# Later window-value stores and residual loads, a sixth pair of value pages, and a later second bank turn for the norm

## The chip, the cores and the metric

The kernel runs on one core of one Trainium2 chip. Its time is device microseconds for one execution; three timed runs of the kernel before gave 931.88, 934.51 and 935.48 us, and the median of such runs is the metric. The profile is of one further execution, which has its own time (below).

## The reference, cut to what matters

One decoder layer is computed for a prompt of 512 positions and for 8 samples of one new position each, whose past of 2048 positions lies in pages of 128 positions, found by a page table. All arithmetic is float32.

```python
q, q_rot, ck, cv, sk, sv, wk, wv, gate, dq, dk, dv = _project(x, pos, attn_norm, w_in)   # RMSNorm, one projection
o_nsa  = gate0 * compressed + gate1 * selected_blocks + gate2 * sliding_window          # 8 heads
o_diff = rmsnorm(softmax(q1 k1) v - lam * softmax(q2 k2) v) * (1 - lam_init)            # 4 heads
x = x + concat(o_nsa, o_diff) @ w_out
x = x + conv_ffn(x)                                                                     # up, conv of width 3, gate, down
y = rmsnorm(x)
```

For the samples the values of the differential heads and of the selected blocks are read page by page, 8 samples x 16 pages. The sliding window keeps 512 positions for each sample: its old values come in shifted by one, the sample's new value row is put in as the last row, the window is used, and the updated window is an output (`s_win_v`).

## The kernel before, in words

TensorE multiplies float32 matrices as split products (a rounded part and a rest, three matmuls), with the 520 columns (512 prompt, 8 sample) in two halves of 260. The work has these stretches in the profiled execution: the input projection together with the scores against the key pages (tiles `kp`, to 174 us); the compressed branch, fed by pages `cp` (to some 314 us); prompt attention together with the value pages `vp` (some 314 to 480 us); the output projection; the up projection, the convolution and the down projection (to the end), which are written out in a fixed order.

Up to the start of the output projection nothing is ordered by hand. Each piece of work is a small process, a Python generator (`p_...`), that yields what it needs: an event, a turn in a ring of buffers (`Ring`, `Slot`), a pause in microseconds, or an operation with its engine and a cost. `Issue.run` builds the order of the instructions from these: it takes the engine that can start first, and on it the operation that is due first. It rehearses 8 times, each time with due times worked back from the rehearsal before, then tries 60 random variations of the best, and emits the program of the best. So one changed pause or one changed turn can move every instruction before the output projection, on all engines. Once emitted, each engine runs its own list in order.

Names that the change and the steps of the prediction touch:

- `p_vload` loads value pages in pairs (`v_load`, line 527 by the helper `page`) into a ring of `NV` buffers `vp` (2 pages, 320 KB each page). All DMAs before the output stage are issued from SyncE (SP), one list.
- `p_win` handles the sliding windows of the 8 samples in order: load the window (L2044, into one of two halves of `kcT`), pause, put the new row in from `vn` (L2046; it has to wait for the window to have landed), pause, store the window to the output (L2048; it has to wait for the row to have landed).
- `p_v` multiplies the pages: `vc<-PTc` opens a sample, `vp,Sd` are the differential heads, `vp,Ss` the selected blocks, `kcT,Sw` the window. Two samples share the one bank of role `v`; `p_half` empties it (tile `od`).
- `p_main` is the prompt attention: per unit, scores (`z,q` and `z,dq`), softmax on VectorE and ScalarE, transposes of the probabilities (`cst,p`, L1896), products with values (`pt,wh`, `pt,wl`, `pt,dv`, `wo,vcp`), and `p_finish`.
- `p_rms`, used by `p_finish` for each of the four differential heads and once for the samples, sums squares on TensorE (`ones,sq`), scales on VectorE, takes the power on GpSimd (tile `rsm`), and spreads the result by transposes (L557). It needs the two small banks of the ring `MR` once each, `m1` and `m2`. A ring gives its turns strictly in the order in which they were asked for: a turn that was asked for holds back all later ones until it is taken.
- `p_residual` loads four tiles of the residual input `xT` into buffers that prompt attention has done with (L2222).
- `numbers`, `load_w`, `win` and the rings `VS` and `VB` are as the quoted code shows.

```python
MR, VB = Ring(2), Ring(1)          # two small banks; one bank for the pages' sums
VS = Ring(NV)                      # pairs of value pages in flight
VR("vp", [128, 2, 640], F32, NV)   # their buffers
```

Of the kernel before, what the change touches and what calls it, by code (L numbers as in the profile page):

```python
# [415 lines left out]
def build(tc, T, plan, last):  # L416
    with tc.manual_schedule():
        _build(tc, T, plan, last)


def _build(tc, T, plan, last):
# [6 lines left out]
    def act(out, in_, func=AF.Copy, **kw):  # L428
        se.activation(out=out, in_=in_, func=func, **kw)  # L429
# [20 lines left out]
    def flat(ap):  # L450
        return ap.rearrange("p a b -> p (a b)")
# [78 lines left out]
    def rms(pool, ssq, n, nt=NT):  # L530


        ssq = ssq if isinstance(ssq, list) else [ssq]
        p = ps("m")
        blk = [(c, min(128, nt - c)) for c in range(0, nt, 128)]
        nb = len(blk)
        sm = pool("rsm", [128, 2, 5], F32, 2)
        if nt % 128:
            ve.memset(sm, 1.0)
        for j, (c, w) in enumerate(blk):  # L540
            for i, s in enumerate(ssq):
                mm(p[:w, j:j + 1], s[:, c:c + w], ones[:, 0:1], i == 0, i == len(ssq) - 1)
        yield None
        full = sum(w == 128 for _, w in blk)
        for lo, hi, w in ((0, full, 128), (full, nb, blk[-1][1])):
            if hi > lo:
                ve.tensor_scalar(out=sm[:w, 0, lo:hi], in0=p[:w, lo:hi], scalar1=1.0 / n, scalar2=EPS,
                                 op0=OP.mult, op1=OP.add)
        yield None
        tt(ge, sm[:, 1, :nb], sm[:, 0, :nb], mhalf[:, :nb], OP.pow)  # L550
        yield None
        out = []
        for j0 in range(0, nb, 4):
            q = ps("m")
            for j in range(j0, min(j0 + 4, nb)):
                w = blk[j][1]
                te.transpose(q[:, (j - j0) * 128:(j - j0) * 128 + w],  # L557
                             sm[:w, 1, j:j + 1].to_broadcast([w, 128]), ident[:w, :w])
            out.append(q)
        yield out  # L560
# [121 lines left out]
    ACC, KB, SR, MR, OR, VB = Ring(4), Ring(2), Ring(4), Ring(2), Ring(1), Ring(1)  # L682
# [5 lines left out]
    def E(*key):  # L688
        return ev.setdefault(key, Event())
# [978 lines left out]
    def p_window():  # L1668
# [17 lines left out]
                       t[:, j * 128:(j + 1) * 128], b4 == 0, b4 == 3)  # L1686
            yield (("pe", 0.24, f), E("wm", b)) + ((ksl,) if b == 0 else ())
        yield ("act", tact(256), lambda: act(flat(Sw), box["p"][:, 0:256])), ksl.done, E("Sw")
    NV = 5
    PL = {}  # L1690


# [90 lines left out]
    PR = [Ring(n) for n in NPR]  # L1783
    VS = Ring(NV)
    PB, PT, W, O = {}, {}, {}, {}
    wslots, vslots = {}, {}

    def v_load(i):
        t = PL["VR"]("vp", [128, 2, 640], F32, NV)
        for n in range(2):  # L1790
            page(t[:, n], T["vpg"], 128 + 2 * i + n)
        vslots[i] = t
# [179 lines left out]
    def p_finish(i):  # L1972
# [23 lines left out]
        yield ("act", tact(512), f), sl  # L1996
        yield ("dve", tdve(512), lambda: ve.tensor_copy(out=box["t"], in_=o), PS), osl.done
        yield from p_rms(box, box["q"], 128, S)

        def f():  # L2000
# [5 lines left out]
        yield f_sub(ol[4 + r][:, :S], box["t"], f32(oh[4 + r][:, :S]), 512), sl.done, E("o", 4 + r)  # L2006

    def p_rms(box, ssq, n, nt):
        m1, m2 = MR.slot(), MR.slot()
        yield m1  # L2010
        g = rms(at, ssq, n, nt)
        yield ("pe", 0.3, lambda: next(g)), m1
        yield ("dve", 0.2, lambda: next(g), PS), m1.done
        yield ("pool", 0.95, lambda: next(g)),
        yield m2
        yield ("pe", 0.46, lambda: box.update(r=next(g))), m2
        box["m"] = m2
# [16 lines left out]
    def win(b):  # L2034
        return kcT[:, 4 * (b % 2):4 * (b % 2) + 4]

    def p_win():

        yield E("kcT", 1)
        yield E("vn")  # L2040
        for b in range(B):
            if b > 1:
                yield E("vb", b - 2)
            yield ("dma", 0.75, lambda: sy.dma_start(out=win(b), in_=T["winv"][b])),  # L2044
            yield 5.0
            yield ("dma", 0.05, lambda: sy.dma_start(out=win(b)[127:128, 3], in_=vn[b:b + 1, 0])), E("win", b)  # L2046
            yield 4.0
            yield ("dma", 0.75, lambda: sy.dma_start(out=T["swv"][b], in_=win(b))),  # L2048

    def p_v():  # L2050
# [60 lines left out]
        def f():  # L2111
            act(o2[:, 0], box["p"][:, 0:32])
            act(o2[:, 1], box["p"][:, 0:32], AF.Square)
        yield ("act", 0.5, f), sl.done
        yield from p_rms(box, o2[:, 1], 128, 32)
        yield (("dve", 0.2, lambda: stt(o2[:, 2], o2[:, 0], lam[:, 7:8], box["r"][0][:, 0:32], OP.mult, OP.mult)),
               box["m"].done)
# [48 lines left out]
    def p_wo_first():  # L2166
# [12 lines left out]
        for m in range(2):  # L2179
            slots = [VS.slot() for _ in range(2)]  # L2180
            for sl in slots:
                yield sl
                sl.got.t = -50.0
            h, l = prep["o", m] = [PL["VR"]("vp", [128, 2, 640], F32R, NV).rearrange("p a b -> p (a b)")[:, 0:1024]
                                   for _ in range(2)]
# [27 lines left out]
    def p_residual():  # L2213

        yield E("outs")
        for m, t, e in ((0, T_SV, E("V", "w")), (1, T_WV, E("V", "w")), (2, T_SK, E("exp", NU - 2, 1, 3)),
                        (3, T_WK, E("exp", NU - 1, 1, 3))):
            yield e

            def f():  # L2220
                xs[m] = P(f"z{t}", [128, NT])
                sy.dma_start(out=xs[m], in_=T["xT"][m])  # L2222
            yield ("dma", 0.8, f),
# [39 lines left out]
    for f, prio in ((p_stage2(), 0), (p_load(), 0), (p_w1v(), 0), (p_split(), 1), (p_product(), 3), (p_group("k"), 2), (p_group("v"), 2), (p_scores(), 2), (p_wload(), -1), (p_window(), 1),  # L2263
                    (p_turned(), 5), (p_vn(), 5), (p_nsa(0), 1), (p_nsa(1), 1), (p_cmp_sample(0), 1),
                    (p_cmp_sample(1), 1), (p_switch(), 0), (p_outs(), -3),
                    (p_vload(), 0), (p_win(), -1), (p_main(), 3),
                    (p_values(), 2), (p_pc(), 2), (p_seq(p_scale, range(NU)), 1),
                    (p_seq(p_turn, range(NU)), 1), (p_seq(p_pv, range(NU)), 0),
                    (p_seq(p_dv, [i for i in range(NU) if units[i][0] == "d"]), 3),
                    (p_seq(p_finish, [i for i in range(NU) if units[i][0] != "s"]), 1), (p_v(), v_prio),  # L2270
                    (p_wo_first(), 4),
                    (p_wo(), 4), (p_residual(), 4),
                    (p_out(0, 0, VB, "v"), 7)):
        Q.spawn(f, prio)
# [271 lines left out]
REHEARSALS, VARIANTS = 8, 60  # L2546
# [27 lines left out]
```

## Time and profile before

| | us |
|---|---|
| median of three runs | 934.51 |
| the profiled execution | 932.64 |
| its span | 930.9 |
| TensorE busy in it | 902.6 (97%) |
| VectorE busy | 572.6 (62%) |
| ScalarE busy | 387.9 (42%) |
| GpSimd busy | 159.5 (17%) |
| waits of TensorE that have a named cause, all stretches | 21.2 |

The span is the stretch that the instructions cover, and 1.7 us of the execution lie around it. TensorE is busy nearly always, so what can be won or lost is in its gaps and in its clock: each row of a table by windows gives, after the busy times, the clock that the throttle granted (1.00 is 2.4 GHz, 0.50 is 1.2 GHz), then the mean busy share of the 16 DMA engines and their rate in GB/s. In a row of a timeline, the first number is the start and the second the length of a merged group; a bracket is the time that the engine had stood before it, and whom it waited for. Matmuls overlap, so lengths of neighbours are not added; the distance of their starts is used.

### The profile page before, as it was taken

To read this page: it belongs to the slowest core of one execution; us is meant where nothing else is said; L and a number is where in the kernel's file an instruction comes from. 1 tells how busy PE (TensorE), PEld (TensorE's weight loads), DVE (VectorE), ACT (ScalarE), POOL (GpSimd) and SP (SyncE) were. 2 spreads that over 40 slices of the span, in tenths; PEclk is the share of its full clock that TensorE was granted. 3 is DMA by queue.
4 is the path that set the end of the run, shared out by engine and by line. 5 is a ranking of instruction groups with operands and counts; after the bars stand their busy time and mean duration, and the time that the engine had idled before them with its cause. 6 is when DMAs were issued, how large, how long until landed. Compare 5 with 4: busy or idle time off the path is not lost.

```text
span 930.9 us, 22292 instructions
## 1 busy us (share of the span) xinstructions
PE 902.6 (97%) x8628; PEld 806.6 (87%) x8628; DVE 572.6 (62%) x1360; ACT 387.9 (42%) x802; POOL 159.5 (17%) x332
## 2 busy tenths in 40 slices
PE   8999999999999999999999999999999999999996
PEld 5998888799999765565569999999999999999996
DVE  7696663365776777776763758777777777321133
ACT  5257331365554665544472234444444444211220
POOL 4220210000100000000012532112111111223230
PEclk9999999989999999999999999999999999999998
DMA  7759999996765689888833332222222222433322
GB/s 262 238 203 343 350 361 348 315 314 214 237 221 179 238 304 345 312 286 306 317 124 134 115 114 92 91 92 91 93 93 97 95 93 72 148 104 106 116 75 93
DMA packets 86061, 179.84 MB, mean 193 GB/s; under 512 B 10049, under 2 KB 28994, under 8 KB 85954
## 3 DMA queue, kind: packets, MB, share of 16 engines
q1 hardware_dynamic: 85954, 178.41, 55.7%
q8 instruction: 68, 1.11, 0.5%
q14 instruction: 39, 0.32, 0.1%
HBM read 165.78 MB, written 12.59 MB: 192 GB/s over the span
## 4 chain that ended last, share of the span: by engine, by line
PE 86%; DMA 6%; SPq 2%; DVE 2%; issue 2%; ACT 1%; POOL 0%; POOLq 0%; DVEq 0%
PE bank L426 83%; DMA vp<-in_vpg 3%; PE bank L1896 2%; DMA kcT<-vn 2%; SPq L527 2%; DMA cp<-in_cpg 1%; DVE xl L438 1%; DMA kp<-in_xT 1%; PE bank L557 0%; DVE y L438 0%; DVE wl L435 0%; ACT gh L429 0%; SPq L625 0%; PE bank L1707 0%; POOL rsm L441 0%
## 5 line engine op out<-in xcount | busy, mean ns | idle before, releaser
L426 PE MATMUL bank<-gl,wh 128*128 128x260 f32 x704 | 199.2, 283 | 0.0
L426 PE MATMUL bank<-gh,wl 128*128 128x260 f32 x704 | 199.1, 283 | 0.0
L426 PE MATMUL bank<-gh,wh 128*128 128x260 f32 x704 | 199.0, 283 | 0.0
L429 ACT ACTIVATE wh<-wr 128x1024 fp32r<-128x1024 f32 (+2 forms) x94 | 96.9, 1031 | 188.3 <-PE bank L426 156.1
L435 DVE TENSOR_TENSOR wl<-wr,wh 128x1024 fp32r<-128x1024 f32 (+1 forms) x86 | 109.5, 1273 | 96.3 <-ACT wh L429 96.0
L426 PEld LDWEIGHTS bank<-gh,wh 128*128 128x128 f32 x704 | 132.7, 188 | 0.0
L426 PEld LDWEIGHTS bank<-gh,wl 128*128 128x128 f32 x704 | 132.6, 188 | 0.0
L426 PEld LDWEIGHTS bank<-gl,wh 128*128 128x128 f32 x704 | 132.6, 188 | 0.0
L426 PE MATMUL bank<-xh,wh 128*128 128x260 f32 (+1 forms) x368 | 105.0, 287 | 1.1 <-ACT wh L429 1.1
L426 PE MATMUL bank<-xl,wh 128*128 128x260 f32 (+1 forms) x368 | 103.9, 284 | 2.2 <-DVE xl L438 2.2
L426 PE MATMUL bank<-xh,wl 128*128 128x260 f32 x352 | 99.6, 283 | 0.0
L426 PE MATMUL bank<-hh,wh 128*128 128x260 f32 (+2 forms) x340 | 96.4, 284 | 0.0
L426 PE MATMUL bank<-hh,wl 128*128 128x260 f32 (+2 forms) x340 | 96.2, 283 | 0.0
L426 PE MATMUL bank<-hl,wh 128*128 128x260 f32 (+2 forms) x340 | 96.1, 283 | 0.0
L426 PEld LDWEIGHTS bank<-xh,wh 128*128 128x128 f32 (+1 forms) x368 | 68.3, 186 | 6.8 <-issue 4.5
L438 DVE SCALAR_TENSOR_TENSOR c<-u,cvw,c 128x536 f32<-128x536 f32 x88 | 69.5, 791 | 2.8 <-ACT c L429 1.3
L426 PEld LDWEIGHTS bank<-xl,wh 128*128 128x128 f32 (+1 forms) x368 | 68.4, 186 | 3.0 <-DVE xl L438 3.0
L426 PEld LDWEIGHTS bank<-xh,wl 128*128 128x128 f32 x352 | 66.4, 189 | 0.1
L435 DVE TENSOR_TENSOR wl<-cp,wh 128x256 fp32r<-128x256 f32 x127 | 47.3, 428 | 29.1 <-ACT wh L429 28.8
L426 PEld LDWEIGHTS bank<-hh,wh 128*128 128x128 f32 x340 | 64.1, 189 | 0.1
L426 PEld LDWEIGHTS bank<-hh,wl 128*128 128x128 f32 x340 | 64.1, 189 | 0.0
L426 PEld LDWEIGHTS bank<-hl,wh 128*128 128x128 f32 x340 | 64.0, 188 | 0.0
(390 smaller groups left out, 1910.5 us busy)
## 6 DMA issues: line engine op xcount, KB each, us to landing
vp<-in_vpg SPq DMA_DIRECT2D x128, 320.0 KB, 5.4
kp<-in_kpg SPq DMA_DIRECT2D x128, 256.0 KB, 5.2
cp<-in_cpg SPq DMA_DIRECT2D x128, 192.0 KB, 3.9
wr<-in_w_up SPq DMA_DIRECT2D x44, 512.0 KB, 3.2
wr<-in_w_in SPq DMA_DIRECT2D x21, 512.0 KB, 5.4
wr<-in_w_down SPq DMA_DIRECT2D x16, 512.0 KB, 3.4
out_zT<-z SPq DMA_DIRECT2D x14, 260.0 KB, 5.5
wr<-in_w_down SPq DMA_DIRECT2D x8, 384.0 KB, 3.1
```

Of the source, the lines that this page charges most:

```text
L426: te.matmul(out, l, r, start=start, stop=stop)
L429: se.activation(out=out, in_=in_, func=func, **kw)
L435: eng.tensor_tensor(out=out, in0=a, in1=b, op=OP.subtract)
L438: ve.scalar_tensor_tensor(out=out, in0=a, scalar=s, in1=b, op0=o0, op1=o1, **kw)
L527: sy.dma_start(out=dst, in_=src[bass.ds(numbers[k][i - k], 1)].rearrange("o p f -> (o p) f"))
L1896: te.transpose(p[:, j * 128:(j + 1) * 128], PB[i, g, q][0][:, k * 128:(k + 1) * 128], ident)
```

## The change

Four edits and what comes of them. The store of a sample's window values waits 10 us instead of 4 us in the plan before it is queued. The ring of value pages has six pairs instead of five. The norm asks for its second small bank after the power instead of together with the first. Residual loads wait 6 us in the plan. A rehearsal that gets stuck no longer throws its plan away for the next.

```diff
-    NV = 5
+    NV = 6
@@ p_rms
-        m1, m2 = MR.slot(), MR.slot()
+        m1 = MR.slot()
         yield m1
         g = rms(at, ssq, n, nt)
         yield ("pe", 0.3, lambda: next(g)), m1
         yield ("dve", 0.2, lambda: next(g), PS), m1.done
         yield ("pool", 0.95, lambda: next(g)),
+        m2 = MR.slot()
         yield m2
         yield ("pe", 0.46, lambda: box.update(r=next(g))), m2
@@ p_win
             yield ("dma", 0.05, lambda: sy.dma_start(out=win(b)[127:128, 3], in_=vn[b:b + 1, 0])), E("win", b)
-            yield 4.0
+            yield 10.0
             yield ("dma", 0.75, lambda: sy.dma_start(out=T["swv"][b], in_=win(b))),
@@ p_residual
             yield e
+            yield 6.0
@@ kernel
-            if k < REHEARSALS:
+            if k < REHEARSALS and p.plan:
                 plan = p.plan
```

Since the order is planned anew, it differs on all five engines up to the output projection; the amount of work is the same. Three places matter.

The list of SP, at the window of the second sample: from its new row (`kcT<-vn`) to the store of that window and the next load. Before:

```order
L2046 DMA kcT_2629<-vn_2640 1x16x8
...
L527 DMA vp_5580<-in_vpg 128x640
...
L527 DMA vp_5600<-in_vpg 128x640
L2048 DMA out_swv<-kcT_2629 128x512
L2044 DMA kcT_2629<-in_winv 128x512
```

Now:

```order
L2047 DMA kcT_2629<-vn_2640 1x16x8
...
L527 DMA vp_5396<-in_vpg 128x640
...
L527 DMA vp_5558<-in_vpg 128x640
L2049 DMA out_swv<-kcT_2629 128x512
L2045 DMA kcT_2629<-in_winv 128x512
```

Each buffer number stands for two page loads, and of the six buffers from vp_5396 to vp_5558 the first and the last are shown. Four page loads stood between the row and the store; now twelve do, for the first five samples alike, four or eight for the last three. Before, it was 8, 4, 8, 4, 10, 4, 6 and none.

The list of TensorE, at the first value pages. `w1vh`, `w1vl` are the last products of the compressed branch, `ce` a small step of the samples' compressed branch, `z10,q0` the first scores of prompt attention. Before:

```order
L426 MATMUL bank5_5000<-kcT_2629,Qzc_81 32x128 x4
L1639 MATMUL bank4_5013<-cst_63,Sw_2635 128x128
L426 MATMUL bank4_5013<-tr_2644,cst_63 128x32
L426 MATMUL bank5_5027<-w2v_2637,hy_4945 128x64 x2
L426 MATMUL bank0_5033<-z10_91,q0_73 128x512
L426 MATMUL bank1_5034<-z10_91,q0_73 128x512
L426 MATMUL bank6_5043<-vc_2630,PTc_2633 32x128
L426 MATMUL bank6_5043<-vp_4794,Sd_103 32x128 x8
L426 MATMUL bank6_5043<-vp_4857,Sd_103 32x128 x8
```

Now:

```order
L1639 MATMUL bank4_4957<-cst_63,Sw_2635 128x128
L426 MATMUL bank4_4957<-tr_2644,cst_63 128x32
L426 MATMUL bank5_4960<-kcT_2629,Qzc_81 32x128 x4
L426 MATMUL bank6_4967<-vc_2630,PTc_2633 32x128
L426 MATMUL bank6_4967<-vp_4841,Sd_103 32x128 x8
L426 MATMUL bank6_4967<-vp_4901,Sd_103 32x128 x8
L426 MATMUL bank6_4967<-vp_4841,Ss_2634 32x128 x2
L426 MATMUL bank6_4967<-vp_4901,Ss_2634 32x128 x2
L426 MATMUL bank6_4967<-vp_4926,Sd_103 32x128 x8
L426 MATMUL bank1_4766<-wh_4773,w1vh1_2656 128x256
```

The first pages were multiplied after all products and after the first unit's scores; now they stand ahead of the last three products and of all scores.

The list of TensorE, at the norm of the last differential head, between its sums of squares (`ones,sq1`) and the transposes of its result (`cst,rsm`). Before:

```order
L426 MATMUL bank5_7340<-ones_67,o2_7307 32x1
L426 MATMUL bank3_7346<-wo_4792,vcp_2631 64x512 x2
L426 MATMUL bank3_7346<-pt_7304,wh_4770 64x512
L426 MATMUL bank3_7346<-pt_7328,wh_4770 64x512
L557 MATMUL bank4_7362<-cst_63,rsm_7341 128x32
L426 MATMUL bank5_7370<-ones_67,sq1_7322 128x1 x4
L557 MATMUL bank4_7385<-cst_63,rsm_7371 128x128 x4
```

Now:

```order
L426 MATMUL bank4_7307<-ones_67,sq1_7288 128x1 x4
L426 MATMUL bank6_6796<-vp_7228,Sd_103 32x128 x8
L426 MATMUL bank6_6796<-vp_7197,Ss_2634 32x128 x2
L426 MATMUL bank6_6796<-vp_7228,Ss_2634 32x128 x2
L426 MATMUL bank3_7331<-wo_4840,vcp_2631 64x512 x2
L426 MATMUL bank3_7331<-pt_7250,wh_4818 64x512
L426 MATMUL bank3_7331<-pt_7314,wh_4818 64x512
L1896 MATMUL bank5_7346<-cst_63,p1_7123 128x128
...
L557 MATMUL bank4_7351<-cst_63,rsm_7308 128x128 x4
```

Nothing stood between the sums and the transposes; now a page, value products and three transposes (one is shown) do, and the transposes use the other small bank, which the norm no longer holds back.

## Rows read from the trace of the kernel before

**Rows 1.** The page: busy time of TensorE, share of the span, instructions.
```profile
PE 902.6 (97%) x8628; PEld 806.6 (87%) x8628; DVE 572.6 (62%) x1360; ACT 387.9 (42%) x802; POOL 159.5 (17%) x332
```

**Rows 2.** Waits of TensorE over the whole span: total us, times, longest us.
```profile
PE bank L426 <- DMA vp<-in_vpg: 3.8, 10, 0.7
PE bank L557 <- POOL rsm L441: 2.5, 2, 1.4
...
PE bank L426 <- DMA cp<-in_cpg: 1.5, 1, 1.5
...
PE bank L426 <- DVE od L438: 1.2, 1, 1.2
...
PE bank L426 <- DVE nsc L441: 1.0, 1, 1.0
PE bank L1896 <- DVE t L438: 1.0, 2, 0.5
```

**Rows 3.** Table by windows of 2 us, 186 to 190 us.
```profile
186.00:188.00 2.00, 2.00 (x9) 0.67 (x9) 1.38 (x3) 1.25 (x4) 0.00 (x0) 0.50 1.03 398
188.00:190.00 2.00, 2.00 (x9) 1.85 (x9) 1.30 (x6) 1.63 (x5) 0.00 (x0) 0.50 1.06 388
```

**Rows 4.** Timeline of TensorE, second and third group of key pages.
```profile
69.55 2.80 PE L426 MATMUL bank<-kp,Qzd 128*32 128x256 f32 x48
...
80.42 2.80 PE L426 MATMUL bank<-kp,Qzd 128*32 128x256 f32 x48
```

**Rows 5.** Table by windows of 2 us, 318 to 322 us.
```profile
318.00:320.00 2.00, 2.00 (x10) 1.67 (x10) 1.97 (x11) 1.18 (x6) 0.00 (x0) 0.50 1.06 408
320.00:322.00 2.00, 2.00 (x11) 0.89 (x10) 0.87 (x2) 0.87 (x5) 0.00 (x0) 0.67 0.81 289
```

**Rows 6.** Timeline of TensorE, last key products of the compressed branch, first value pages.
```profile
302.44 0.29 PE L426 MATMUL bank<-wl,w1h 128*128 128x256 f32 x1
302.56 0.29 PE L426 MATMUL bank<-wh,w1l 128*128 128x256 f32 x1
...
325.09 0.30 PE L426 MATMUL bank<-vc,PTc 128*32 128x128 f32 x1
...
325.24 1.02 PE L426 MATMUL bank<-vp,Sd 128*32 128x128 f32 x28
...
326.34 1.01 PE L426 MATMUL bank<-vp,Sd 128*32 128x128 f32 x28
```

**Rows 7.** Timeline of SP: start, length, DMAs issued.
```profile
306.76 5.71 SPq L527 DMA_DIRECT2D vp<-in_vpg  x10
...
352.16 0.53 SPq L2046 DMA_DIRECT2D kcT<-vn  x1
352.89 2.51 SPq L527 DMA_DIRECT2D vp<-in_vpg  x4
357.75 0.35 SPq L2048 DMA_DIRECT2D out_swv<-kcT  x1
```

**Rows 8.** The page's DMA issues: KB each, median us to landing.
```profile
vp<-in_vpg SPq DMA_DIRECT2D x128, 320.0 KB, 5.4
```

**Rows 9.** Table by windows of 10 us, 350 to 390 us.
```profile
350.00:360.00 10.00, 8.71 (x96) 4.36 (x93) 8.07 (x28) 5.69 (x18) 0.00 (x0) 1.00 1.03 390
...
380.00:390.00 10.00, 8.75 (x109) 4.16 (x101) 5.36 (x18) 3.59 (x9) 0.00 (x0) 1.00 0.92 303
```

**Rows 10.** Groups of TensorE by line, 325 to 488 us: count, busy us, mean ns.
```profile
L1896 PE MATMUL bank<-cst,p 128*128 128x128 f32 x199 | 34.1, 290 | 1.2 <-DVE t L438 1.0 <-ACT pt L429 0.2
L426 PE MATMUL bank<-z,q 64*128 64x512 f32 (+3 forms) x114 | 21.5, 468 | 0.0
...
L426 PE MATMUL bank<-pt,wh 128*64 128x512 f32 (+3 forms) x64 | 11.9, 476 | 0.0
```

**Rows 11.** Timeline of TensorE, norm of the last differential head.
```profile
474.51 1.05 PE L426 MATMUL bank<-ones,sq 128*128 128x1 f32 x8
476.99 0.65 PE L557 MATMUL bank<-cst,rsm 128*128 128x128 f32 x4 [1.43 <-POOL rsm L441]
```

**Rows 12.** Table by windows of 2 us, 478 to 482 us.
```profile
478.00:480.00 2.00, 1.52 (x8) 1.19 (x8) 1.65 (x3) 0.98 (x2) 0.48 (x1) 0.59 0.08 29
480.00:482.00 2.00, 2.00 (x11) 0.93 (x12) 0.90 (x2) 1.94 (x5) 0.00 (x0) 0.56 0.00 0
```

## The prediction

> **What bounds the kernel now.** I read the page first: TensorE is busy for 902.6 us, 97% of the span, and no other engine above 62% [rows 1]. The amount of work does not change, so the time can change only through gaps of TensorE, through its clock, or through the place of work that would otherwise be waited for. The list of TensorE's waits says how much there is [rows 2]: value pages 3.8 us in ten waits of at most 0.7, the power of the norm 2.5 in two, the bank that holds the pages' sums (`od`) 1.2, a small step of the selected blocks (`nsc`) 1.0, the bank behind the norm (`t`) 1.0, the first compressed pages 1.5. Then I read the tables by windows for the clock. Behind three of the longer gaps TensorE runs at 1.2 GHz for a while: behind the wait for compressed pages [rows 3], behind the wait for `nsc` [rows 5], and behind the norm of the last head [rows 12]. At a granted 0.50 a stretch of 2 us does 1 us of work less, so the second fall costs 2 x 0.50 + 2 x 0.33 = 1.7 us and the third 2 x 0.41 + 2 x 0.44 = 1.7 us. Only these stretches, from the end of the key pages to the end of prompt attention, hold anything that the change can reach; the feed-forward part is written out and stays.
>
> All sums are against the profiled execution, 932.64 us, which is span 930.9 and 1.7 around it. It lies 1.9 us under the median of 934.51; I apply the difference to the median.
>
> **The change part by part.**
>
> *Stores set back.* In the list of SP the store of a window waits for the new row to land. Row and store show it: the row goes out at 352.16, four pages follow until 355.40, and the store leaves only at 357.75; nothing behind it leaves either [rows 7]. With twelve pages ahead of the store this hold goes, since at 5.71 us for ten issues [rows 7] twelve take 6.9 us even when no buffer holds them, longer than the 5.4 us that a page takes to land [rows 8]. What is late next is the buffer of a page, not the queue. The window half that is stored is needed again two samples later, so the later store holds nobody. The residual tiles are first needed in the output projection, behind all pages; their pause costs nothing, and one landing of 5.4 us [rows 8] if that cover went.
>
> *Six pairs.* Two more pages can be under way, 12 for 10. Beyond the 3.8 us of page waits [rows 2] this can win nothing directly. I count all 3.8 as gone where SP is the cause, and set a new cost against it.
>
> *Pages start earlier.* The order has them ahead of the last products. The last product that holds their first buffer starts at 302.56; before, the first page was issued 4.2 us later [rows 6, 7] and used at 325.24. Now, by the rows of the list, TensorE reaches the first page after 45 more products at 0.12 us [rows 6], 5.4 us, and ten small groups of about 0.5 us, so 10.3 us behind that product. From there to the end of the third sample stand 48 pages at 1.10 us for four [rows 6], 13.2 us, and between them 30 score matmuls at 2 x 21.5 / 114 = 0.38, 37 transposes at 34.1 / 199 = 0.17, 14 value products at about 2 x 11.9 / 64 = 0.37 [rows 10] (the trace counts scores and value products twice), and some 3 us of small steps: 13.2 + 11.3 + 6.3 + 5.2 + 3 = 39 us. TensorE alone would be through at 49.3 us. The pages: a rate of 390 GB/s makes 0.84 us of the 320 KB, one of 303 GB/s makes 1.08 [rows 8, 9]. The lower one was measured while a store held SP, the higher one at a full DMA share, so I take 0.90. First landing at 0.3 + 5.4, 47 more at 0.90, and three windows in and out, 0.5 MB each, 1.4 us each: 52.2 us. That is 2.9 us behind TensorE, of which I count 2.5 as waits; at 0.84 it is nothing, at 1.08 it is 12.4 us. Net for the value pages: -3.8 + 2.5 = -1.3 us.
>
> The Trainium skill, DMA: Bandwidth & Descriptors, section Bandwidth, puts the memory's share for one core at about 358 GB/s when both cores of a pair stream, as a limit below the fabric's. By it a page takes 0.92 us and the three windows 1.5 each, 53.4 us in all, 1.2 us more of waiting. The windows with 388 to 408 GB/s [rows 3, 5] are above it, so the trace doesn't agree with it as a limit here, where one core runs.
>
> *Gap at the start of prompt attention.* The chain of the selected blocks now has its steps among the products: between the two small transposes that `nsc` stands behind lie twelve products and four transposes, 1.9 us, where six products, 0.7 us, lay. The wait of 1.0 [rows 2] goes, and with it, I think, the 1.7 us of lower clock: -2.7. The bound on the other side is 0, if the page waits make the clock fall in the same place.
>
> *Samples' bank.* Samples 2 and 3 share a bank with 0 and 1, which must be emptied. Before, nothing stood between; now the transpose of the window and three others do, about 0.9 us: -0.8 of 1.2 [rows 2].
>
> *Norm.* From the sums of squares of the last head to its transposes the chain took 2.48 us, 1.43 of them idle [rows 11]. Now a page, four value products and three transposes stand there, some 3.4 us by the same rows: the wait of 1.4 goes. The wait for `t`, 0.5, goes where the transposes use the other bank. The fall of the clock, 1.7, should go too. That is 3.6; I take 3.0, since the last heads' other transposes still follow softmax closely. The other norms of the heads had no wait.
>
> *First compressed pages.* Behind the last key page now stand 42 projection matmuls for 33, 1.1 us more cover for the wait of 1.5 [rows 2]. But the first key pages are used 30 matmuls, 3.6 us, later, and between the second group and the first only 65 stand for 80: pages that came 10.9 us apart [rows 4] must come a little faster. From -1.1, with the clock's fall of at least 2.0 us [rows 3] as much again, to +2; I take -0.5.
>
> *What the new order brings with it.* A planned order never fits the chip quite; the waits that I take away were of this kind. In the old order they were `od` 1.2, `nsc` 1.0, `t` 1.0 and the norm 1.4 [rows 2], 4.6 us, and I expect as much of others in the new one.
>
> Sum: -1.3 - 2.7 - 0.8 - 3.0 - 0.5 + 4.6 = -3.7 us. 932.64 becomes 928.9, and the median 934.5 becomes 930.8.
>
> **The rivals.**
>
> The new order is as good as it looks: no other waits come, -8.3, 926.2 us. For it: most of the named gaps get more cover than they were long. Against it: every order of this planner has small waits.
>
> The waits only move: what goes here returns elsewhere, to 8.3 us, 934.5 us. For it: no work is removed, and TensorE is at 97%. Against it: the queue's hold and the ring's hold are real and go.
>
> Slower: the page supply becomes the bound at the start. Place: the first three samples, where TensorE would like 48 pages in 39 us. At 303 GB/s [rows 9] the waiting is 12.4 in place of 2.5, so -3.7 + 9.9 = +6.2, 940.7 us. It decides from about 1.00 us a page, where the waiting reaches 7.2 us and the gain is eaten up. For it: DMA share 1.03 with the rate at 390 [rows 9], there is no more to be had. Against it: the store no longer stops the queue, and the samples that follow have more other work between their pages.
>
> The clock falls at the pages. In the trace page waits of up to 0.7 us leave the granted clock at 1.00 [rows 2, 9], and falls came only behind gaps of 1.0 us or more. Now more pages lie one behind the other at the start, and three falls of 1.7 us would make -3.7 + 5.1 = +1.4, 935.9 us. The Trainium skill, TensorE: Matmul & The Clock Gate, section HAM oscillation, describes bursts of matmuls between DMA waits where every burst starts at the lower clock; so far the trace does not agree for the short waits.
>
> **How the numbers follow.** My forecast has 0.40, with a range of its own of 928 to 933.5. As good as it looks 0.20, waits only move 0.22, page supply 0.10, clock at the pages 0.08. A measurement of this kernel can tell 0.5%, 4.7 us, from no change: faster means under 929.8, slower over 939.2. Faster are all of the second case and nearly half of the first, 0.37; slower is most of the page supply, 0.09; the rest, 0.54, is no change. The range leaves out a tenth on either side: 925 to 938.5.
>
> **What would show it.** Right: the store of a window leaves without SP standing, no wait of a microsecond or more for the norm's power before the output projection, a granted clock of 1.00 at the start of prompt attention and at its end, page waits of 2 to 3 us together, mostly for the first three samples. Wrong: page waits over 7 us, a fall of the clock between the first pages and the fourth sample, or key pages waited for in the input projection.

## The result, and the profile after

The changed kernel took 922.84 us, the median of four runs (921.75 to 925.21), beside 933.91 us of the kernel before (931.88 to 935.48): a ratio of 0.9885, with a 95% interval of 0.9856 to 0.9914. That is 11 us less. The forecast was 930.8 us with a range of 925 to 938.5: the direction was right, but the time lies below the range. Four far slower executions among the experiments below, of 1241 to 3013 us, are left out of their ratios.

The profiled execution took 923.06 us, with a span of 921.2 us, 9.7 less than before. The page of the changed kernel, busy times as in [rows 1]:

```profile
PE 899.1 (98%) x8628; PEld 805.7 (87%) x8628; DVE 573.5 (62%) x1362; ACT 384.4 (42%) x790; POOL 168.3 (18%) x342
```

The work of TensorE is the same (8628 matmuls), its busy time 3.5 us shorter. Its waits after, beside [rows 2] (total us, times, longest):

```profile
PE bank L426 <- DVE z L441: 1.4, 2, 1.2
...
PE bank L426 <- DMA cp<-in_cpg: 1.3, 2, 1.0
...
PE bank L426 <- ACT p L429: 1.1, 1, 1.1
PE bank L426 <- DMA kp<-in_kpg: 1.0, 2, 0.8
PE bank L557 <- POOL rsm L441: 1.0, 1, 1.0
...
PE bank L426 <- DMA vp<-in_vpg: 0.8, 3, 0.4
PE bank L426 <- DVE od L438: 0.5, 1, 0.5
...
PE bank L426 <- DVE nsc L441: 0.2, 1, 0.2
```

Value pages fell from 3.8 to 0.8, the power of the norm from 2.5 in two waits to 1.0 in one (that of the last norm of the whole kernel, at 914 us, is left), `od` from 1.2 to 0.5, `nsc` from 1.0 to 0.2, and `t` is gone. New are 1.1 for the probabilities of the first scores (`p`, 0.2 before) and 1.0 for key pages. The whole list adds up to 15.2 us, against 21.2 before.

SP after, at the window of the second sample, which [rows 7] shows before: start, length, DMAs issued.

```profile
338.46 0.54 SPq L2047 DMA_DIRECT2D kcT<-vn  x1
340.25 8.84 SPq L527 DMA_DIRECT2D vp<-in_vpg  x12
349.13 0.43 SPq L2049 DMA_DIRECT2D out_swv<-kcT  x1
349.61 0.43 SPq L2045 DMA_DIRECT2D kcT<-in_winv  x1
```

Twelve pages follow the row, and the store leaves right behind the last: SP no longer stands at it. TensorE at the start of prompt attention, first value pages and what it waited for, beside [rows 6]:

```profile
307.66 0.28 PE L426 MATMUL bank<-wh,w1l 128*128 128x256 f32 x1
...
318.92 0.30 PE L426 MATMUL bank<-vp,Sd 128*32 128x128 f32 x3
...
326.55 0.42 PE L426 MATMUL bank<-vp,Sd 128*32 128x128 f32 x8 [0.17 <-DMA vp<-in_vpg]
327.36 0.43 PE L426 MATMUL bank<-vp,Sd 128*32 128x128 f32 x8 [0.39 <-DMA vp<-in_vpg]
328.90 1.13 PE L426 MATMUL bank<-z,q 64*128 64x512 f32 x4 [1.11 <-ACT p L429]
```

The first page is multiplied 11.3 us behind the last `w1l` product (318.92 - 307.66). The three gaps in brackets make 1.7 us together. The table by windows of 2 us, with the columns of [rows 3, 5, 12], at the places that these show: compressed branch, start and end of prompt attention.

```profile
186.00:188.00 2.00, 0.95 (x7) 0.51 (x6) 0.00 (x0) 0.96 (x1) 0.00 (x0) 0.71 0.98 340
188.00:190.00 2.00, 2.00 (x9) 0.96 (x9) 1.76 (x5) 0.88 (x5) 0.00 (x0) 0.50 1.03 403
...
318.00:320.00 2.00, 2.00 (x52) 1.96 (x52) 0.47 (x3) 0.63 (x3) 0.00 (x0) 1.00 1.04 406
...
326.00:328.00 2.00, 1.23 (x32) 0.42 (x21) 1.85 (x12) 0.99 (x5) 0.00 (x0) 1.00 0.96 312
328.00:330.00 2.00, 1.10 (x8) 0.35 (x11) 1.93 (x7) 0.84 (x4) 0.00 (x0) 1.00 0.90 298
...
478.00:480.00 2.00, 2.00 (x17) 1.75 (x15) 0.00 (x0) 0.92 (x2) 0.00 (x0) 1.00 0.00 0
```

The fall behind the compressed pages is still there; those at the start and the end of prompt attention are gone. The table by windows of 10 us, beside [rows 9]:

```profile
330.00:340.00 10.00, 9.82 (x171) 6.98 (x170) 9.69 (x44) 7.60 (x27) 0.93 (x1) 1.00 1.03 383
...
350.00:360.00 10.00, 10.00 (x144) 6.03 (x142) 8.20 (x27) 4.20 (x13) 0.00 (x0) 1.00 0.99 376
...
380.00:390.00 10.00, 10.00 (x149) 6.74 (x147) 7.02 (x25) 5.08 (x16) 1.87 (x3) 1.00 0.68 225
```

In the last two TensorE is busy without a gap, and by 380 the pages are ahead: the share of the DMA engines is 0.68 where it was 0.92. A page still takes 5.5 us to land (median; 5.4 before [rows 8]). The norm of the last differential head on TensorE, start and length, beside [rows 11]:

```profile
463.05 0.95 PE L426 MATMUL bank<-ones,sq 128*128 128x1 f32 x8
...
466.97 0.60 PE L557 MATMUL bank<-cst,rsm 128*128 128x128 f32 x4
```

The chain now has 3.9 us and TensorE does not stand. Of the groups of [rows 10] the transposes show best that the work itself costs what it did (count, busy us, mean ns, idle before):

```profile
L1896 PE MATMUL bank<-cst,p 128*128 128x128 f32 x200 | 33.6, 286 | 0.5 <-ACT pt L429 0.3 <-DVE pt L1910 0.2
```

They cost 286 ns each for 290, with 0.5 us of waits for 1.2.

The up projection starts at 527.0 us, 536.9 before, so the whole gain lies ahead of it. For each kernel below I added up, from windows of 2 us up to that start, the time in which TensorE was not busy (idle) and the busy time times one minus the granted clock (clock):

| stretch, us | before: idle + clock | after: idle + clock |
|---|---|---|
| 0-60 | 5.0 + 0 | 4.6 + 1.5 |
| 60-200 | 1.5 + 3.0 | 2.3 + 3.1 |
| 200-300 | 0.2 + 0 | 0 + 0 |
| 300-340 | 1.9 + 1.7 | 2.2 + 0 |
| 340-460 | 6.0 + 0 | 1.5 + 0 |
| 460-500 | 2.5 + 1.5 | 1.5 + 0 |
| 500 on | 2.8 + 0 | 1.4 + 0 |
| sum | 19.8 + 6.2 | 13.5 + 4.6 |
| rest (busy, at full clock) | 510.9 | 508.9 |

So 6.3 us of idle time, 1.6 of lower clock and 2.0 of busy time make the 9.9.

### The profile page after: what moved, and what is told of

It reads as the page before. It is cut to its first block, busy times and chain, and to the rows that moved or that the text cites. A ratio compares the mean times of both kernels' runs of the same rounds, so it can differ in the third digit from the quotient of the medians.

```text
span 921.2 us, 22310 instructions
## 1 busy us (share of the span) xinstructions
PE 899.1 (98%) x8628; PEld 805.7 (87%) x8628; DVE 573.5 (62%) x1362; ACT 384.4 (42%) x790; POOL 168.3 (18%) x342
## 3 DMA queue, kind: packets, MB, share of 16 engines
q8 instruction: 68, 1.11, 0.5%
## 4 chain that ended last, share of the span: by engine, by line
PE 89%; DMA 4%; DVE 3%; issue 2%; SPq 1%; ACT 1%; POOL 0%; POOLq 0%; DVEq 0%
PE bank L426 85%; PE bank L1896 3%; DMA kp<-in_kpg 2%; SPq L527 1%; DMA kcT<-vn 1%; DVE bank L1835 1%; DMA cp<-in_cpg 1%; DMA wr<-in_w_in 0%; PE bank L557 0%; DMA vp<-in_vpg 0%; DVE y L438 0%; PE bank L1707 0%; DVE wl L435 0%; ACT gh L429 0%; ACT xh L429 0%
## 5 line engine op out<-in xcount | busy, mean ns | idle before, releaser
L441 DVE TENSOR_TENSOR u<-bank,rst 128x260 f32<-128x260 f32 x132 | 40.0, 333 | 38.6 <-PE bank L426 33.0
```

The costliest lines, as they stand in the source:

```text
L441: eng.tensor_tensor(out=out, in0=a, in1=b, op=op)
```

## The experiments

The planner makes a new order after every edit. So the first question is what an edit is worth, and what the order that was drawn happens to be worth. All ratios are to the kernel before, on the same chip.

**One edit at a time.** Each kernel is the one before with one of the four edits and the line on the stuck rehearsal (by itself that line leaves the program as it was, word for word); the edits are those of the diff of the change, one at a time, as here in store_alone:

```diff
-            yield 4.0
+            yield 10.0
             yield ("dma", 0.75, lambda: sy.dma_start(out=T["swv"][b], in_=win(b))),
```

> Theory 1, each edit removes its own hold: TensorE's page waits fall from 3.8 us to about 1.5, SP's hold at the window stores from 10.2 us to under 2, the norm's wait of 1.4 and the lower clock at the end of prompt attention stay; 931 us against 933.9. Theory 2, the new time is a draw of the planner, whatever the edit: the time lies anywhere from 926 to 938, and waits that the edit doesn't touch (start of prompt attention, norm) move as much as those it touches.

> Theory 1, each edit removes its own hold: SP's hold at the window stores stays at some 10 us, but two more pages in flight hide part of it, page waits 3.8 to about 2.5 us; the norm's wait and the fall of the clock at the end stay; 932.5 us against 933.9. Theory 2, a draw of the planner: anywhere from 926 to 938, with the untouched waits changed as well.

> Theory 1, each edit removes its own hold: the wait for the power ahead of the output projection (1.4 us), the one behind it (0.5) and the fall of the clock there (1.5) go, page waits stay at 3.8; 930.5 us against 933.9. Theory 2, a draw of the planner: anywhere from 926 to 938, page waits and the start of prompt attention changed too.

> Theory 1, each edit removes its own hold: a load that is needed 30 us later is moved, so nothing: 933.9 us, within 1. Theory 2, a draw of the planner: the order differs on all engines, so the time lies anywhere from 926 to 938; a change of 3 us or more here can only be the draw.

| kernel | us | ratio | 95% |
|---|---|---|---|
| store_alone | 927.28 | 0.9928 | 0.9904 to 0.9952 |
| six_alone | 930.87 | 0.9970 | 0.9949 to 0.9991 |
| norm_alone | 928.77 | 0.9938 | 0.9919 to 0.9957 |
| resid_alone | 929.52 | 0.9947 | 0.9922 to 0.9971 |

All four are faster, 2.2% taken together, nearly twice what they give in common. Even the pause of the residual loads, for which SP stands 4.8 us with and without it, "gives" 0.5%. In all four the norm of the last head is no longer waited for, edited or not: only the 1.0 of the kernel's last norm is left. So that wait belonged to the one order of the kernel before. What looks like an edit's own effect is the page supply. Page waits are 1.2 us in store_alone and 1.6 in six_alone, lower than was expected of either, but 5.6 in norm_alone and 3.2 in resid_alone, where 3.8 would have stayed. In store_alone the stores hold SP for 2.8 us, in six_alone for 15.3 in seven waits. The row of SP's waits in the kernel before (total us, times, longest):

```profile
SPq L2048 <- DMA kcT<-vn: 10.2, 4, 3.8
```

the same row in store_alone:

```profile
SPq L2048 <- DMA kcT<-vn: 2.8, 1, 2.8
```

and in six_alone:

```profile
SPq L2048 <- DMA kcT<-vn: 15.3, 7, 2.9
```

But the gap for `nsc` is larger with three of the edits alone, 2.0 us in store_alone, six_alone and norm_alone, and 1.4 in resid_alone, where before had 1.0.

**Other draws of the same kernel.** The random variations of the planner get another seed, once with the source of before and once with that of after:

```diff
-    rng = np.random.default_rng(0)
+    rng = np.random.default_rng(1)
```

> The kernel before with another seed of the planner's random variations, no edit. Theory 1, each edit removes its own hold, and the order before is a fair one: within 2 us of the kernel before, and the norm's wait stays. Theory 2, the order before was a poor draw: clearly faster, 928 to 932 us, without the norm's wait and with the window store still holding SP for 10 us or more, as in the four single edits.

> As with the other seed. Theory 1: within 2 us of the kernel before. Theory 2: 928 to 932 us, and the norm's wait gone; the two seeds differ from each other by 1 to 3 us.

> The kernel before, another seed. If the order before was a poor draw and the edits are worth little: 927 to 932 us, as the first two other seeds (932.0 and 928.5) and the single edits. If the order before was typical: 933 to 936 us.

> As the seed before it: 927 to 932 us if the order before was a poor draw, 933 to 936 us if it was typical.

> The changed kernel with another seed. Theory 1: within 2 us of the changed kernel's 922.8, page waits about 1 us. Theory 2, if the changed order was also a good draw: 924 to 929 us. A mixture is likeliest: the edits are worth some 4 us between the means of the seeds, the draw of the kernel before the rest.

> As with the other seed: theory 1 within 2 us of 922.8, theory 2 from 924 to 929 us; page waits about 1 us and no store that holds SP by both.

> The changed kernel, another seed. If the edits are worth some 3 us by themselves: 924 to 928 us, and the mean over the seeds of the changed kernel stays some 3 us under that of the kernel before. If only the draw counts: 927 to 932 us, as its first two other seeds (929.0 and 929.8), and the means over the seeds without the first come together.

> As the seed before it: 924 to 928 us if the edits are worth some 3 us by themselves, 927 to 932 us if only the draw counts.

| seed | before: ratio (95%) | lost, us | after: ratio (95%) | lost, us |
|---|---|---|---|---|
| 0 (as given) | 1 | 26.0 | 0.9885 (0.9856 to 0.9914) | 18.1 |
| 1 | 0.9963 (0.9943 to 0.9984) | 27.8 | 0.9946 (0.9924 to 0.9967) | 19.1 |
| 2 | 0.9934 (0.9914 to 0.9954) | 23.4 | 0.9951 (0.9926 to 0.9976) | 22.8 |
| 3 | 0.9976 (0.9952 to 1.0000) | 25.2 | 0.9946 (0.9926 to 0.9966) | 22.6 |
| 4 | 0.9978 (0.9958 to 0.9999) | 24.0 | 0.9946 (0.9918 to 0.9974) | 21.6 |

"Lost" is idle plus clock from the table's method, one profile for each. The four other seeds have a mean of 0.9963 without the edits and 0.9947 with them. So, as a bookkeeping by these means, of the 1.15%, 0.37% (3.4 us) is that before's own order is worse than its other draws, 0.16% (1.5 us) is the edits on draws that nobody chose, and 0.62% (5.8 us) is that the changed kernel's own order is better than other draws of the same source. Seed 2 alone even stands the other way round (0.9934 and 0.9951), so 0.16% is not certain to differ from zero.

The profiles say where edits and draw part. From 300 to 340 us the loss is 3.3 to 8.6 us on the five orders without the edits and 1.1 to 2.2 on the five with them; from 460 to 500 us it is 0.7 to 4.0 and 0 to 1.5. These two stretches go with the edits: the gap for `nsc` (0.3 to 2.0 us without) shows on none of the four other seeds with them. How they close it is not shown. It is not by the stores alone, which hold SP for 9.0 to 13.9 us without the edits and for 0 to 4.1 with them: in store_alone they hold it for 2.8 us, and 6.1 us are still lost from 300 to 340 us. Part is given back in two places: 200 to 300 us has 1.3 to 1.8 on the other seeds with the edits (0.2 to 0.7 without), and 340 to 460 us has 4.6 to 5.9 (3.3 to 6.0 without). Of these ten only the order of the changed kernel has 1.5 there. On average over seeds 1 to 4, 6.5 us are won in the first two stretches and 2.7 given back in the other two. All in all the lost time falls by 3.6 us (25.1 to 21.5), and the up projection starts 2.4 us earlier. That is more than the 1.5 us of the ratios, so that the edits' own worth stays uncertain by a microsecond or more. Page waits, without the edits 3.8, 5.0, 2.4, 3.4 and 2.6 us, are 3.7, 3.9, 2.8 and 3.2 on the other seeds with them, where about 1 was expected, and 0.8 in the changed kernel alone.

**The due times kept.** The last emission takes other settings than the rehearsals, so the due times stay and only what the edit itself moves differs:

```diff
-    NV = 6
+    NV = OPT["pairs"]
...
+BEFORE = dict(pairs=5, store=4.0, resid=0.0, late=False)
+AFTER = dict(pairs=6, store=10.0, resid=6.0, late=True)
...
+        OPT.update(dict(AFTER, pairs=5) if k == REHEARSALS + VARIANTS else AFTER)
```

(The pauses and the turn of the norm read `OPT` in the same way; shown is newplan_five, and the last line is what differs between the five.)

oldplan_edits is before's due times with all edits; newplan_plain is after's due times with none; newplan_store4, newplan_early and newplan_five take back one edit each (the store's pause, the late turn of the norm, the sixth pair).

> The search is made for the kernel before, and only the program that is emitted has all edits, at the due times of that plan. If the edits are worth something by themselves: page waits from 3.8 to about 1.5 us, the window stores hold SP no more, 931 to 932 us against some 934.8. If only the draw counts: the waits at the start of prompt attention and at the norm stay with the plan, 934 to 935 us.

> The search is made for the changed kernel, and the emitted program has none of the edits. If the edits are worth something by themselves: stores hold SP for 10 us again, page waits 3 us and more, some 3 to 4 us over the changed kernel's 922.8, so 926 to 927. If only the draw counts: within 1 us of 922.8, because start of prompt attention and norm keep the order of that plan.

> The changed kernel's plan, with the store's pause alone put back to 4 us in the emitted program. If the store is what the edits are worth: SP held for 8 us or more at the stores, page waits 2 us and more, 925 to 926 us. If only the draw counts: within 1 us of 922.8.

> The changed kernel's plan, with the norm asking for both banks at once in the emitted program. If the norm's turn counts by itself: transposes wait behind its second turn for the power, 1 to 2 us for each of four heads, of which some 2 us show, 925 us. If only the draw counts: within 1 us of 922.8, and no wait for the power before the output projection.

> The due times that the changed kernel ended with, all of its edits but one: five pairs of value pages in place of six. Theory (the gain hangs on the exact order, and any small disturbance of it loses some 5 us): 0.993 to 0.996, TensorE's lost time between 340 and 460 us back at 3 to 6 us from 1.5. Rival (each edit has its own steady worth, and the sixth pair is worth the 0.3% that it had alone): 0.991 to 0.992.

| kernel | us | ratio | 95% | lost, us |
|---|---|---|---|---|
| oldplan_edits | 930.99 | 0.9954 | 0.9930 to 0.9977 | 24.4 |
| newplan_plain | 929.16 | 0.9954 | 0.9940 to 0.9968 | 21.8 |
| newplan_store4 | 928.97 | 0.9948 | 0.9926 to 0.9969 | 21.6 |
| newplan_early | 927.51 | 0.9942 | 0.9921 to 0.9963 | 21.4 |
| newplan_five | 928.15 | 0.9929 | 0.9912 to 0.9945 | 24.6 |

At the due times of before, the edits do much of what they were made for: in oldplan_edits no store waits for its row any more, page waits are 2.4 us for 3.8, and neither the norm of the last head nor `t` is waited for. The waits for `nsc` (1.0) and `od` (1.2) stay with the plan. That is worth 0.46%, about as the first of its two expectations had it.

At the due times of after, the first three kernels (newplan_five came later) came out slower than either of their expectations, which went up to 927 us for newplan_plain, 926 for newplan_store4 and 925 for newplan_early. Taking back any one of the three edits that were tried loses 0.4 to 0.6%, and taking back all four 0.7%. (The pause of the residual loads was not tried alone.) If each had a worth of its own, three of them would already make 1.6%. So their worths do not add, and each is needed for the time of this order. That what is lost is the fit of the order, which any of them disturbs, is the likeliest reading, but it is not shown: no run disturbs these due times without taking back an edit. For the store at least it is not the hold of SP that comes back. With the pause at 4 us and these due times, six loads still stand between row and store for the first sample and ten for the next four, and no store waits for its row, where 8 us of hold or more was expected. SP in newplan_store4 at the second sample:

```profile
336.73 0.51 SPq L2048 DMA_DIRECT2D kcT<-vn  x1
337.43 8.48 SPq L527 DMA_DIRECT2D vp<-in_vpg  x10
345.96 0.43 SPq L2050 DMA_DIRECT2D out_swv<-kcT  x1
```

Its up projection starts 6.9 us later than in the changed kernel: 3.5 of these are lost time, most of it from 300 to 340 us (2.6), and 3.4 are busy time at full clock.

In newplan_five one can see a cause. TensorE's waits for value pages in it (total us, times, longest):

```profile
PE bank L426 <- DMA vp<-in_vpg: 5.0, 7, 1.9
```

and in the changed kernel, run beside it:

```profile
PE bank L426 <- DMA vp<-in_vpg: 1.0, 3, 0.5
```

The timeline of SP in newplan_five ahead of the longest of them (start, length, DMAs issued):

```profile
427.96 0.75 SPq L2206 DMA_DIRECT2D wo<-in_w_out  x1
436.31 3.89 SPq L527 DMA_DIRECT2D vp<-in_vpg  x6
```

its timeline of TensorE at that wait:

```profile
442.10 0.43 PE L426 MATMUL bank<-vp,Sd 128*32 128x128 f32 x8 [1.89 <-DMA vp<-in_vpg]
```

and its table by windows behind it (the granted clock is the third number from the end):

```profile
442.00:444.00 2.00, 1.90 (x13) 1.11 (x15) 0.56 (x1) 0.00 (x0) 0.00 (x0) 0.64 0.99 368
444.00:446.00 2.00, 2.00 (x7) 0.51 (x3) 0.65 (x3) 0.00 (x0) 0.00 (x0) 0.51 0.86 301
```

With five pairs SP stands for 7.6 us until a buffer is free. A page issued at 436.31 lands at 441.7 by the median of 5.4 [rows 8], and TensorE, which waits 1.89 us, goes on at 442.10, soon at 1.2 GHz. From 340 to 460 us this kernel loses 4.7 + 3.4 us, the changed one 1.4. With six pairs SP stands there too, but only for 5.6 us, from 424.98 to 430.60, and no page wait of TensorE is over 0.5 us. SP in the changed kernel, run again:

```profile
424.39 0.59 SPq L2205 DMA_DIRECT2D wo<-in_w_out  x1
430.60 3.09 SPq L527 DMA_DIRECT2D vp<-in_vpg  x4
```

The sixth pair is thus worth its 4.8 us in this order. In six_alone, in another order, the same edit gave 0.3%, no more than a new seed does. By its ratio this run does not choose between the two expectations: 0.9929 lies between them, and its interval covers both. What it shows is the place: the loss from 340 to 460 us is back, at 8.1 us even more than the 3 to 6 expected.

**The changed kernel again.** It ran once more, unaltered, on the chip of newplan_five.

> The changed kernel once more, unaltered, beside the kernel before on one chip, in five rounds. Theory (the order that the changed kernel drew is itself better than other draws with the same edits by some 0.6%): again a ratio of 0.987 to 0.990. Rival (the first measurement of 0.9885 was favourable and the order is like the other draws): 0.993 to 0.996.

923.32 us, ratio 0.9888 (0.9871 to 0.9906). The first measurement was no lucky one, and the order itself is better than its fellows, whose ratios lie at 0.9946 to 0.9951.

## Why the prediction was wrong

Its terms, beside what the two profiled executions show (waits and clock of the place that the term names):

| term of the sum | forecast | measured |
|---|---|---|
| value pages | -1.3 | -3.0 (3.8 to 0.8) |
| start of prompt attention | -2.7 | -3.0 (`nsc` 0.8, clock 1.7, `ce` 0.5) |
| samples' bank | -0.8 | -0.7 |
| norm | -3.0 | -3.5 (1.5, `t` 0.5, clock 1.5) |
| first compressed pages | -0.5 | +0.9 (`cp` -0.2, `kp` +1.0, clock +0.1) |
| what the new order brings | +4.6 | +1.2 (`p` 0.9, `m` 0.3) and clock +1.5 in the first 60 us |
| not in the sum | | -1.3 (small waits), -2.0 (busy time) |
| sum | -3.7 | -9.9 |

- **The step that failed is "What the new order brings with it".** It took the waits that before had had (4.6 us) as what any order has. The new order brought 1.2 us in such waits, and 1.0 more for key pages, a risk that the prediction had under its own term. The 1.5 us of clock in the first 60 us are no part of it: the second profile of the same program has none there. Of the five terms that were read from the order itself four were right in sign, and three within 0.5 us. The lump was the one term with no place in the program.
- **The total fits other draws.** With seeds 1 to 4 the edits give 0.9947, or 929.6 us of 934.51, 1.2 below the forecast: there something is given back, at 200 to 300 and 340 to 460 us. The forecast was thus near a usual order of these edits, while the order at hand was to be seen. In part that is luck: its terms do not fit there one by one (page waits are 3.4 us on average, not 2.5).
- **The value pages were mis-sized too.** The sum took 0.90 us a page and 2.5 us of new waits. At 383 GB/s, as measured from 330 to 340 us, a page of 320 KB takes 0.86; the bound at 0.84 had no wait, and 0.8 came. The step about TensorE's side held: the first page was to be used 10.3 us behind the last product and was at 11.3. The Trainium skill, DMA: Bandwidth & Descriptors, section Bandwidth, gives about 358 GB/s for each core when both of a pair stream. As a limit here, where one core runs, it would have made the pages dearer, and the trace does not agree with it: the windows above have 383 and 376 GB/s over 10 us each.
- **The first compressed pages went the other way.** The prediction saw that key pages would have to come faster and put the risk at up to +2. They were waited for, 0.8 us at the third group and 0.3 later, which it had named as a sign of being wrong, and the better cover of the compressed pages gave only 0.2 us for the 1.1 that it counted.
- **The gap at the start changed its cause.** The wait for `nsc` went as forecast, and one of 1.1 us for `p` came, with 0.6 for pages, all between 326 and 330 us. Idle time there is no less than before (2.2 for 1.9); the gain is that the clock stayed at 1.00.
- **The norm: right in size, wrong in cause.** The 1.4 us went, but the later second turn was not needed for it: the wait is gone in newplan_early, at the same due times with the early turn, and in all the other runs with the early turn but before itself. (newplan_plain has 0.7 us at an earlier head.) The fall of the clock was read as 1.7 us and is 1.5, because TensorE was busy for only 1.52 of the first 2 us [rows 12].
- **The rivals.** Page supply and the clock at the pages did not come: no page wait over 0.4 us, and a granted clock of 1.00 from 300 us to the output projection. (By the prediction's own sum the page supply would have eaten up the gain at 6.2 us of waits, 3.7 + 2.5, not 7.2.) "The waits only move" did not hold for this order. "As good as it looks", 926.2, was nearest and still 3.4 too high. In the two profiled executions the change is -9.9 for its -8.3: page waits gave 1.7 us more, busy time 2.0 and small waits 1.3, the start, the samples' bank and the norm 0.7 together; new waits and clock took 2.7 back, compressed and key pages 1.4.

Two things stay open. Why this order fits the chip better than its fellows beyond the page waits was not taken apart. And the busy time at full clock, 507 to 512 us over all these orders for the same matmuls, is a spread as large as the effect, which no run here explains.

## What to carry to other kernels

Where a planner makes a new order after each edit, time some other seeds of both versions first: here a new seed alone moved the time by 0.2 to 0.7%, more than the edits did on average over the other seeds. Read the waits of the order that will run and price those with a place; what has no place belongs into the range and not into the sum. One edit by itself says little in such a program: four edits alone gave 2.2%, all together 1.15%, of which about 0.2% is theirs on other draws; at the due times of before they gave 0.46%.

## What was not expected of the hardware

The length of a gap does not tell whether TensorE's clock falls. Two gaps of about a microsecond cost a fall: 1.04 us for `nsc` in the kernel before, with 0.50 granted at 318 us [rows 5], and one for compressed pages in the changed kernel, with 0.50 at 188 us. TensorE's timeline in the kernel before:

```profile
315.79 0.35 PE L426 MATMUL bank<-nsc,cst 128*128 128x2 f32 x2 [1.04 <-DVE nsc L441]
```

and in the changed kernel:

```profile
187.48 2.17 PE L426 MATMUL bank<-cp,Qzs 128*32 128x128 f32 x8 [1.05 <-DMA cp<-in_cpg]
```

One of 1.11 us at 328 us in the changed kernel, with two shorter ones just ahead, cost none, and neither did this one in the kernel before, whose granted clock stays at 1.00 from 340 to 460 us (the clock part of that stretch is 0 in the table above); TensorE's timeline of before:

```profile
359.37 0.27 PE L426 MATMUL bank<-vc,PTc 128*32 128x128 f32 x1 [1.19 <-DVE od L438]
```

Gaps of 1.44 and 1.89 us in newplan_five each cost a fall (0.69 and 0.50 in the windows from 394 us, 0.64 and 0.51 from 442 us).

Two executions of the same program differ at the same place. In the first profile of the changed kernel the clock falls behind a gap of 1.00 us near its start (timeline of TensorE, then table by windows of 2 us):

```profile
11.06 0.39 PE L426 MATMUL bank<-xl,wh 128*128 128x260 f32 x1 [1.00 <-DVE xl L438]
```

```profile
14.00:16.00 2.00, 1.96 (x10) 1.56 (x8) 2.00 (x3) 0.61 (x2) 1.34 (x1) 0.50 1.08 400
```

In its second profile the gap there is longer, and the clock stays at 1.00:

```profile
11.45 0.39 PE L426 MATMUL bank<-xl,wh 128*128 128x260 f32 x1 [1.58 <-DVE xl L438]
```

```profile
14.00:16.00 2.00, 1.14 (x8) 0.78 (x6) 2.00 (x2) 1.28 (x3) 1.66 (x2) 1.00 1.06 396
```
